# The first stage of a diffusion transformer kernel: an order written out for four queues, and a norm whose modulation enters as ScalarE's scale and bias

## The chip, the cores and the metric

The kernel runs on one core of a Trainium2 chip. Time is device time in microseconds (us) of one launch, the median of several runs. The profile is one further execution, taken by the hardware profiler. The core's engines are TensorE (PE in the profile; PEld is its weight load), VectorE (DVE), ScalarE (ACT), GpSimd (POOL) and SyncE (SP, which issues most DMAs). Each has its own queue of instructions that it takes strictly in the order of the program; semaphores join them.

## What is computed

Two blocks of a transformer with adaptive norms, in float32. Each sublayer is preceded by an RMS norm whose result is scaled and shifted by a modulation that is a matrix product of the conditioning vector:

```python
def _rms(t, g):
    y = t32 * lax.rsqrt(jnp.mean(t32 * t32, axis=-1, keepdims=True) + NORM_EPS)
    return y.astype(t.dtype) * g
def _modulate(t, g, shift, scale):
    return _rms(t, g) * (1 + scale) + shift
def _swiglu(h, w13, w2):
    gte, up = jnp.split(h @ w13, 2, axis=-1)
    return (jax.nn.silu(gte) * up) @ w2
...
mod = (jax.nn.silu(c) @ mod_w[i] + mod_b[i]).reshape(bsz, 3, 3, 1, D_MODEL)
lat = lat + 0.5 * mod[:, 0, 2] * _swiglu(_modulate(lat, norm_g[i, 0], mod[:, 0, 0], mod[:, 0, 1]), ffn_w13[i, 0], ffn_w2[i, 0])
```

There are 256 tokens of the sequence (`lat`) and 256 of a context (`cx`) with a modulation of its own; the model width is 1024 and the hidden width of the feed-forward 2816. The sublayers are: feed-forward, convolution mixer, feed-forward; feed-forward, attention, feed-forward.

## The kernel before

**Layout.** Activations are held transposed: 128 partitions of the model width by 512 columns (256 of the sequence, s=0, and 256 of the context, s=1), in eight slices k=0..7. So a modulation is one value per partition for each k and s. Products keep float32 accuracy by splitting: an operand becomes a high part (`hh`, `wh`), rounded to the type that PE takes at full rate, and a low part (`hl`, `wl`), the difference; each product is three matmuls, high by high, high by low and low by high (lines 122 to 124). `split` makes the high part on ACT (L98) and the low part on DVE (L99).

**First stage.** It ends where the fourth block of the first feed-forward's weights starts; it takes three blocks (i=0..2), each with a gate and an up result of 512 columns. Nothing can be multiplied before x has come, its squares are summed, and the first modulation is known. The stage is cut into quarters q=0..3 of two slices k each, so that products can start with the first quarter. The steps in `FIRST_STEPS` are written out for PE:

- `P` ch q (`mod_pe`, L758): the product of the conditioning with 256 columns of the modulation's weights (ch 1 is the scale, ch 0 the shift), in two halves that each wait for their own 512 KB load; then a copy of the row to SBUF on ACT (L763).
- `T` ch q (`mod_turn`, L770): small matmuls that turn the row into columns; DVE adds the bias and writes A00 (scale, L775) or B00 (shift, L775).
- `F` (`fill`, L731): matmuls without use that keep PE busy; `WARM` of them stand at the start.
- `W` i (`first_w`): the load of weight block i and its split in four parts.
- `N` q (`norm_q`): DVE multiplies A00 by the norm's weight (L784); for each k and s DVE makes t = x * A * (1/rms) (L264), ACT makes hh = t + B (L274), DVE makes hl = (t + B) - hh (L275).
- `H` q (`copy_q`): ACT writes the unsplit t + B to `h32` (L798), which sums of halves need later.
- `M` i q: the twelve products of block i with quarter q.
- `S`: the conditioning vectors broadcast over the partitions (`scbc`) and their Silu on ACT.

1/rms over all partitions (`rms_all`, L252, copied by L845) is made ahead of P00. Only PE's order is fixed (`manual_schedule` with PE alone). DVE, ACT and SP get their order from the framework's scheduler.

**Behind it.** `w13_post` makes silu(gate) * up of the three blocks and splits it. `h.sums()` adds and subtracts halves of h32 and splits the results (T1 to T4), which the blocks from 8 on use in place of h (products on sums of halves, seven instead of eight). `tick(n)` gives n units of modulation work to DVE: each (L142) is a row-wise product of a 1024-wide piece of modulation weights with `scbc`. Ticks stand behind every block and every finished output of the second product (`ev` of them each). Blocks 3 to 7 take h as it is (`AS_IS`), in `ffn`. Five constants (`convk`, `qg`, `kg`, `cosT`, `sinT`) are loaded through ACT's DMA queue.

**DMA.** SP issues the loads in its order, and each waits for the one before it on the same of eight semaphores; ACT's loads take from the same eight.

Of the kernel before, what the change touches and what calls it, by code (L numbers as in the profile page):

```python
# [9 lines left out]
F32 = mybir.dt.float32  # L10
# [15 lines left out]
HEADS = 8  # L26
KVH = 2
EPS = 1e-6
WARM = 36
FILL = 8  # L30

FIRST_STEPS = (
    "P10 P00 T10 T00 N0 F W0 M00 W1 P11 P01 T11 T01 N1 H0 M10 W2 M01 P12 H1 M11 P02 T12 T02 "
    "N2 M20 H2 M21 P13 P03 T13 T03 N3 M02 M12 M22 H3 M03 M13 M23 S"
)


# [1 line left out]
def hybrid_kernel(ctx: ExitStack, tc: tile.TileContext, a: dict, out: bass.AP):  # L42
# [53 lines left out]

    def split(hi, lo, src):
        nc.scalar.activation(out=hi, in_=src, func=AF.Copy)  # L98
        nc.vector.tensor_tensor(out=lo, in0=src, in1=hi.bitcast(F32), op=ALU.subtract)  # L99

    def half():

# [515 lines left out]
    def ffn(l, b, h, tot, gate, tail, gs=(), ev=1.5):  # L618
        gs = list(gs)
        i0 = 0  # L620
        for t, n in enumerate(THIRDS):
            between = ()
            if tot == T2:
                heads = []
                if t == 0 and not gs:

                    w = [load_w(a["w13"][l, b, 0])]
                    gs = [new_pair("g") for _ in range(2)]
                    pp = [(psum("pg"), psum("pu")) for _ in range(2)]
                    w13_mm(pp[0], w[0], h, range(KT), 0, S)  # L630
                    flush()
                    w.append(load_w(a["w13"][l, b, 1]))
                    w13_mm(pp[1], w[1], h, range(KT), 0, S)
                    h.sums(0)
                    w13_mm(pp[0], w[0], h, range(KT), S, T2)
                    w13_post(pp[0], gs[0], 0, T2)
                    heads.append(Pair(a["w13"][l, b, 2], h))
                    h.sums(1)
                    heads[0].sums(0)
                    w13_mm(pp[1], w[1], h, range(KT), S, T2)  # L640
                    w13_post(pp[1], gs[1], 0, T2)
                    heads[0].head()
                    h.sums(2)
                    heads[0].sums(1)
                prev = None
                for i in range(len(gs), n):
                    if t == 0 and not heads and i in AS_IS[l, b]:
                        w = load_w(a["w13"][l, b, i])
                        pp = psum("pg"), psum("pu")
                        if prev:  # L650
                            prev.seven()
                        w13_mm(pp, w, h, range(4), 0, T2)
                        if prev:
                            gs.append(new_pair("g"))
                            prev.four(gs[-1])
                            prev = None
                        w13_mm(pp, w, h, range(4, KT), 0, T2)
                        gs.append(new_pair("g"))
                        w13_post(pp, gs[-1], 0, T2)
                        tick(4)  # L660
                        continue
                    if heads:
                        pr = heads.pop(0)
                    else:
                        pr = Pair(a["w13"][l, b, i0 + i], h)
# [12 lines left out]

                def last():
                    gs.append(new_pair("g"))  # L680
                    prev.four(gs[-1])

                between = (prev.seven, last) if prev else ()
            else:
                for i in range(n):
                    w = load_w(a["w13"][l, b, i0 + i])
                    gs.append(new_pair("g"))
                    pp = psum("pg"), psum("pu")
                    w13_mm(pp, w, h, range(KT), 0, tot)
                    w13_post(pp, gs[i], 0, tot)  # L690
                    tick(1)
            i0 += n
            box = {}

            def ws2(m):
                if m // 2 not in box:
                    src = a["w2a"][l, b, m // 2] if t == 0 else a["w2b"][l, b, t - 1, m // 2]
                    box[m // 2] = load_raw(src, 2 * n * P)
                raw = box[m // 2]
                o = (m % 2) * n * P  # L700
                hi, lo = half()
                split(hi[:, : n * P], lo[:, : n * P], raw[:, o : o + n * P])
                return lambda k: (hi[:, k * P : k * P + P], lo[:, k * P : k * P + P])

            cur = gs
            end = t == len(THIRDS) - 1
            project(
                ws2, lambda k, c0, c1: (cur[k][0][:, c0:c1], cur[k][1][:, c0:c1]), n,
                gate, tail if end else None, tot, 2 if end and tot == T2 else 0, ev, between,
            )  # L710
            gs = []
# [32 lines left out]

    rows = {}

    def mod_pe(ch, q):


        raws = []  # L750
        for i in range(2):
            raws.append(hot("pm", F32))
            nc.sync.dma_start(raws[i], a["mod0"][ch, q, :, i * 1024 : i * 1024 + 1024])
        pr = psum("pr") if (ch, q) == (1, 0) else psmall("pr")
        for k in range(KT):
            g = 32 * (k % 4)
# [22 lines left out]
            op=ALU.add,  # L779
        )  # L780

    def norm_q(q):
        k2 = slice(2 * q, 2 * q + 2)
        nc.vector.tensor_tensor(  # L784
            out=A00[:, k2, :], in0=A00[:, k2, :], in1=both(normg[:, 0, 0, k2]), op=ALU.mult
        )
        for k in range(2 * q, 2 * q + 2):
            for s in range(2):
                t = None
                if k % 2:  # L790
                    t = tp.tile([P, T2], F32, name=nm("t"), tag="sg", bufs=3)[:, :S]
                ts[k, s] = norm_k(s, k, h, A00, B00, ris[s], t)

    def copy_q(q):
        for s in range(2):
            h32[q, s] = gp.tile([P, T2], F32, name=nm("hr"), tag="gl" if s else "gh")
            for k in range(2 * q, 2 * q + 2):
                nc.scalar.activation(  # L798
                    out=h32[q, s][:, (k % 2) * S : (k % 2) * S + S], in_=ts[k, s],
                    func=AF.Identity, bias=B00[:, k, s : s + 1],  # L800
                )

    pps = {}
    ris, ts = [], {}

    def first_mm(i, q):
        if q == 0:
            pps[i] = psum("pg"), psum("pu")
        w13_mm(pps[i], ws[i], h, range(2 * q, 2 * q + 2), 0, T2)

    ws, gs0 = {}, []

    def load_sc():
        for v in range(2):
            nc.sync.dma_start(scbc[:, v, :], a["c2"][v : v + 1, :].to_broadcast([P, D]))
            nc.scalar.activation(out=scbc[:, v, :], in_=scbc[:, v, :], func=AF.Silu)

    def first_w(i):
        if i < 2:
            ws[i] = load_w(a["w13"][0, 0, i], fine=True)  # L820
            return
        raw = load_raw(a["w13"][0, 0, i])
        parts = [new_pair("w") for _ in range(4)]
        for j in (0, 2, 1, 3):
            split(*parts[j], raw[:, j * T2 : j * T2 + T2])
        ws[i] = lambda o: tuple(t[:, o % T2 : o % T2 + P] for t in parts[o // T2])

    steps = {
        "P": mod_pe,
        "T": mod_turn,  # L830
        "F": lambda: fill(FILL),
        "H": copy_q,
        "S": load_sc,
        "W": first_w,
        "N": norm_q,
        "M": first_mm,
    }
    with tc.manual_schedule(engines={mybir.EngineType.PE}):
        fill(WARM)
        sums = [rms_sum(s, (accs[s], accs[s, "last"])) for s in range(2)]  # L840
        for step in FIRST_STEPS.split():
            if step == "P00":
                for s in range(2):
                    ris.append(tp.tile([P, S], F32, name=nm("ris"), tag=f"ris{s}", bufs=1))
                    nc.scalar.copy(ris[s], rms_all(*sums[s]))  # L845
            steps[step[0]](*(int(c) for c in step[1:]))
    done[0, 0] = done[0, 1] = 16
    h = FirstBlocks(h, h32)
    for i in range(3):
        gs0.append(new_pair("g"))  # L850
        w13_post(pps[i], gs0[i], 0, T2)
    h.sums()
    tick(4)

    convk = cload("convk", [P, 3, KT])
    qg = cload("qg", [P, 1])
    kg = cload("kg", [P, 1])
    cosT = cload("cosT", [P, S])
    sinT = cload("sinT", [P, S])


    hn = Plain()
    ffn(0, 0, h, T2, lazy_gate(0, 0), tail_norm(0, 1, hn), gs0, 1.8)
    h = hn

    zs = []
# [358 lines left out]
```

## Time and profile before

| | us |
|---|---|
| median of 3 runs | 1588.35 |
| lowest and highest | 1585.33, 1588.66 |
| profiled execution, whole | 1586.51 |
| its span (first to last instruction) | 1584.7 |

The mean granted clock of TensorE over the profiled execution is 0.995 of full speed.

How to read the lines. In the busy times by stretch, the columns are the stretch, its length, then busy us and number of instructions of PE, PEld, DVE, ACT and POOL, then the granted clock of TensorE, the share of the DMA engines and GB/s. In the rows in time, the columns are start, duration, engine, line of the code, operation, result and operands, shapes and count; brackets give idle time before it and what ended it. A matmul of float32 operands shows as two records, one of the rounded type as one; rows of PE last longer than the distance to the next, as matmuls are pipelined. In the groups by shape, the columns behind the count are busy us in all, mean ns of one, and idle us before it with what ended it. In the list of waits they are us in all, times, and the longest.

### The profile page before, as it was taken

The page shows a single profiled execution, that of the slowest core. Times are in us where ns is not written, and L with a number is a line of the kernel's source. Part 1 is how long each engine was busy: PE and PEld are TensorE (multiplying, and loading weights), DVE is VectorE, ACT ScalarE, POOL GpSimd, SP SyncE. Part 2 cuts the span into 40 slices and gives each one's busy share as a digit, 9 for nine tenths or more (in the row PEclk, how much of TensorE's full clock was granted, in tenths as well). Part 3 has the DMA queues.
Part 4 walks back from the last instruction along what each step waited for, and adds up shares of the span by engine and source line. Part 5 has one row for each costly group of instructions (what it writes and reads, how often), then busy time and mean ns, then how long its engine had stood idle before and what let it go on. Part 6 is the DMA issues. An engine that isn't in the chain of part 4 may idle for free.

```text
span 1584.7 us, 25774 instructions
## 1 busy us (share of the span) xinstructions
PE 1565.9 (99%) x10666; PEld 1448.4 (91%) x10666; DVE 1302.0 (82%) x1984; ACT 720.4 (45%) x1103; POOL 26.1 (2%) x20
## 2 busy tenths in 40 slices
PE   9999999999999999999999999999999998999999
PEld 6788998999888899999899899899899897899999
DVE  5988789979988789898898899788898788665554
ACT  6522452545322365335255376245255456543443
POOL 0000000000000000000000000000000004100000
PEclk9999999999999999999999999999999999999999
DMA  9565235334454423442433423532543554355452
GB/s 361 200 221 186 94 137 183 120 132 158 170 205 160 159 81 132 144 151 100 174 139 110 161 87 109 184 135 98 196 147 127 206 190 163 105 199 191 161 202 102
DMA packets 39573, 248.78 MB, mean 157 GB/s; under 512 B 5408, under 2 KB 7200, under 8 KB 14624
## 3 DMA queue, kind: packets, MB, share of 16 engines
q1 hardware_dynamic: 36864, 245.38, 44.1%
q10 hardware_dynamic: 2592, 1.76, 0.4%
q8 instruction: 83, 1.36, 0.3%
q14 instruction: 34, 0.28, 0.1%
HBM read 244.77 MB, written 1.05 MB: 155 GB/s over the span
## 4 chain that ended last, share of the span: by engine, by line
PE 94%; DVE 2%; ACT 2%; DMA 1%; issue 0%; ACTq 0%; DVEq 0%
PE py L123 10%; PE py L124 10%; PE py L122 10%; PE p L124 7%; PE p L123 7%; PE p L122 7%; PE q L122 5%; PE q L124 5%; PE q L123 5%; PE pg L122 3%; PE pg L124 3%; PE pg L123 3%; PE pu L122 3%; PE pu L123 3%; PE pu L124 3%; PE pv L122 1%
## 5 line engine op out<-in xcount | busy, mean ns | idle before, releaser
L98 ACT ACTIVATE wh<-wr 128x1024 fp32r<-128x1024 f32 (+2 forms) x276 | 276.7, 1013 | 374.3 <-PE py L123 123.2
L99 DVE TENSOR_TENSOR wl<-wr,wh 128x1024 fp32r<-128x1024 f32 (+2 forms) x276 | 320.4, 1166 | 94.2 <-ACT wh L98 93.5
L142 DVE CUSTOM_DVE_ANT_0 junk<-wr,scbc,modb 128x1024 bf16<-128x1024 f32 x224 | 286.7, 1280 | 32.8 <-DMA wr<-in_modT 30.2
L122 PE MATMUL py<-gh,wh 128*128 128x512 f32 (+1 forms) x746 | 263.2, 353 | 0.0
L123 PE MATMUL py<-gl,wh 128*128 128x512 f32 (+1 forms) x746 | 263.0, 353 | 0.0
L124 PE MATMUL py<-gh,wl 128*128 128x512 f32 (+1 forms) x746 | 262.8, 352 | 0.0
L124 PEld LDWEIGHTS py<-gh,wl 128*128 128x128 f32 x746 | 141.1, 189 | 19.0
L122 PEld LDWEIGHTS py<-gh,wh 128*128 128x128 f32 x746 | 141.2, 189 | 18.5
L123 PEld LDWEIGHTS py<-gl,wh 128*128 128x128 f32 x746 | 141.2, 189 | 18.2
L99 DVE TENSOR_TENSOR wl<-ws,wh 128x1024 fp32r<-128x1024 f32 x108 | 131.7, 1222 | 26.9 <-ACT wh L98 26.5
L98 ACT ACTIVATE wh<-ws 128x1024 fp32r<-128x1024 f32 x108 | 113.7, 1058 | 79.6 <-PE p L123 33.8
L124 PE MATMUL p<-th,wl 128*128 128x256 f32 x432 | 122.2, 283 | 0.0
L123 PE MATMUL p<-tl,wh 128*128 128x256 f32 x432 | 122.2, 283 | 0.0
L122 PE MATMUL p<-th,wh 128*128 128x256 f32 x432 | 122.2, 283 | 0.0
L453 DVE SCALAR_TENSOR_TENSOR x<-py,G,x 128x256 f32<-128x256 f32 x168 | 74.2, 477 | 27.2 <-PE py L124 27.0
L122 PE MATMUL q<-bh,wh 128*128 128x256 f32 x320 | 90.6, 283 | 0.0
L123 PE MATMUL q<-bl,wh 128*128 128x256 f32 x320 | 90.6, 283 | 0.0
L124 PE MATMUL q<-bh,wl 128*128 128x256 f32 x320 | 90.6, 283 | 0.0
L122 PEld LDWEIGHTS p<-th,wh 128*128 128x128 f32 x432 | 82.9, 192 | 0.3
L123 PEld LDWEIGHTS p<-tl,wh 128*128 128x128 f32 x432 | 82.9, 192 | 0.3
L124 PEld LDWEIGHTS p<-th,wl 128*128 128x128 f32 x432 | 82.9, 192 | 0.0
L122 PE MATMUL pg<-hh,wh 128*128 128x256 f32 (+1 forms) x240 | 76.0, 317 | 2.7 <-ACT wh L98 1.6
(236 smaller groups left out, 4037.3 us busy)
## 6 DMA issues: line engine op xcount, KB each, us to landing
wr<-in_w SPq DMA_DIRECT2D x88, 1024.0 KB, 4.9
wr<-in_modT SPq DMA_DIRECT2D x64, 1024.0 KB, 4.9
wr<-in_w2b SPq DMA_DIRECT2D x32, 896.0 KB, 4.6
wr<-in_w2a SPq DMA_DIRECT2D x16, 1024.0 KB, 4.9
pm<-in_mod SPq DMA_DIRECT2D x16, 512.0 KB, 9.6
wr<-in_cw_cx SPq DMA_DIRECT2D x8, 1024.0 KB, 4.9
wr<-in_cw_b SPq DMA_DIRECT2D x4, 1024.0 KB, 5.9
wr<-in_cw_out SPq DMA_DIRECT2D x4, 1024.0 KB, 4.8
```

Of the source, the lines that this page charges most:

```text
L98: nc.scalar.activation(out=hi, in_=src, func=AF.Copy)
L99: nc.vector.tensor_tensor(out=lo, in0=src, in1=hi.bitcast(F32), op=ALU.subtract)
L122: nc.tensor.matmul(ps, wh, mh, start=first, stop=False, **kw)
L123: nc.tensor.matmul(ps, wh, ml, start=False, stop=False, **kw)
L124: nc.tensor.matmul(ps, wl, mh, start=False, stop=last, **kw)
L142: nc.vector.tensor_tensor_reduce(out=junk, in0=raw[:, j * D : j * D + D], in1=scbc[:, v, :], scale=1.0, scalar=modb[:, l, col : col + 1], ...
L453: nc.vector.scalar_tensor_tensor(out=x[:, m, s * S : s * S + S], in0=ps[:, o : o + S], scalar=g[:, m, s : s + 1], in1=x[:, m, s * S : s * ...
```

## The change

- **Order.** `FIRST_STEPS` is written anew, and `manual_schedule` now holds PE, DVE, ACT and SP: all four take the stage's work in the order of the steps. Loads become steps of their own (`L` for modulation weights, `R` for weight blocks), splits are cut into single parts (`W` i p), and the products of the first two blocks with quarter 0 into single kinds (`h` high by high, `w` with the low weight, `l` with the low activation; arguments block, quarter, slice). The other `M` steps go through each slice as h, w, l, gate and up by turns.
- **Norm.** `U` q: DVE makes x * (norm's weight) * (1/rms) straight into h32, which needs no modulation. `N` q j then makes hh = A * that + B on ACT with scale and bias per partition; the unsplit value in place, for q=0 on DVE (`tensor_scalar`), otherwise on ACT with scale and bias; and hl as a difference of two tensors on DVE. The product of A00 with the norm's weight is gone.
- **Place of other work.** `X` (1/rms) stands between P10 and P00. The two loads of `scbc` come behind all loads of the stage; the constants' loads come behind the Silu of `scbc`. `h.sums()` is called in the first of the blocks of `ffn`, its instructions held behind the last low weight split of block 1. `tick(4)` behind it is gone, and `ev` of the first feed-forward is 2 where it was 1.8.
- **Filler.** `WARM` is 34 where it was 36, `FILL` 4 where it was 8.

```diff
+FIRST_STEPS = (
+    "L10 L00 R0 R1 P10 X U0 L11 P00 L01 T10 T00 W00 N00 W01 N01 F h000 w000 l000 R2 W10 W11 "
+    "h001 w001 h100 h101 l001 l100 l101 W02 W03 U1 P11 L12 P01 L02 T11 T01 w100 w101 N10 N11 "
+    "W12 W13 M01 W20 W21 U2 W22 W23 P12 L13 P02 L03 T12 T02 M11 N20 N21 M20 U3 P13 P03 T13 "
+    "T03 M21 N30 N31 M02 M12 M22 M03 M13 M23 S"
+)
...
+                        if "T1" not in h.t:
+                            with tc.issue_after(rows["W1"]):
+                                h.sums()
                         w13_mm(pp, w, h, range(4), 0, T2)
...
+    def scale_q(q):
+        for s in range(2):
+            h32[q, s] = gp.tile([P, T2], F32, name=nm("hr"), tag="gl" if s else "gh")
         for k in range(2 * q, 2 * q + 2):
             for s in range(2):
...
+                nc.vector.scalar_tensor_tensor(
+                    out=raw_of(k, s), in0=x[:, k, s * S : s * S + S],
+                    scalar=normg[:, 0, 0, k : k + 1], in1=ris[s], op0=ALU.mult, op1=ALU.mult,
+                )
+
+    def norm_one(q, j):
+        k = 2 * q + j
+        hs = [pick(h, k, s * S, s * S + S) for s in range(2)]
+        ab = [(A00[:, k, s : s + 1], B00[:, k, s : s + 1]) for s in range(2)]
         for s in range(2):
...
+            nc.scalar.activation(
+                out=hs[s][0], in_=raw_of(k, s), func=AF.Identity, scale=ab[s][0], bias=ab[s][1]
+            )
+        for s in range(2):
+            r = raw_of(k, s)
+            if q == 0:
+                nc.vector.tensor_scalar(
+                    out=r, in0=r, scalar1=ab[s][0], scalar2=ab[s][1], op0=ALU.mult, op1=ALU.add
+                )
+            else:
                 nc.scalar.activation(
...
+                    out=r, in_=r, func=AF.Identity, scale=ab[s][0], bias=ab[s][1]
                 )
+        for s in range(2):
+            nc.vector.tensor_tensor(
+                out=hs[s][1], in0=raw_of(k, s), in1=hs[s][0].bitcast(F32), op=ALU.subtract
+            )
...
+    queues = [nc.tensor, nc.vector, nc.scalar, nc.sync]
+    with tc.manual_schedule(engines={e.engine for e in queues}):
         fill(WARM)
...
-    h.sums()
-    tick(4)
...
-    ffn(0, 0, h, T2, lazy_gate(0, 0), tail_norm(0, 1, hn), gs0, 1.8)
+    ffn(0, 0, h, T2, lazy_gate(0, 0), tail_norm(0, 1, hn), gs0, 2)
```

In the order that follows from it, ACT takes in quarter 0: the first weight part, hh, hh, a weight part, hh, hh, then two weight parts of block 1 and the other two of block 0; in quarter 1: hh, hh, unsplit, unsplit, twice over, then six weight parts, then the row copies of quarter 2. DVE takes the four units of block 3's tick behind the five sums and ahead of the splits of the sums.

More of the change, by code (lines that the diff above doesn't have):

```diff
@@ L28 @@
 EPS = 1e-6
-WARM = 36
-FILL = 8
+WARM = 34
+FILL = 4
 FIRST_STEPS = (
-    "P10 P00 T10 T00 N0 F W0 M00 W1 P11 P01 T11 T01 N1 H0 M10 W2 M01 P12 H1 M11 P02 T12 T02 "
-    "N2 M20 H2 M21 P13 P03 T13 T03 N3 M02 M12 M22 H3 M03 M13 M23 S"
[4 rows of a table added]
 )
@@ L98, in split @@
         nc.scalar.activation(out=hi, in_=src, func=AF.Copy)
-        nc.vector.tensor_tensor(out=lo, in0=src, in1=hi.bitcast(F32), op=ALU.subtract)
+        return nc.vector.tensor_tensor(out=lo, in0=src, in1=hi.bitcast(F32), op=ALU.subtract)
     def half():
@@ L745, in hybrid_kernel, with mod_load @@
     rows = {}
+    def mod_load(ch, q):
+        rows[ch, q] = [hot("pm", F32) for _ in range(2)]
+        for i in range(2):
+            nc.sync.dma_start(rows[ch, q][i], a["mod0"][ch, q, :, i * 1024 : i * 1024 + 1024])
     def mod_pe(ch, q):
[L750 to L753, printed above, removed]
+        raws = rows[ch, q]
         pr = psum("pr") if (ch, q) == (1, 0) else psmall("pr")
@@ L780, in mod_turn, with first_inv, raw_of @@
         )
[L782 to L786, printed above, removed]
+    def first_inv():
+        for s in range(2):
+            ris.append(tp.tile([P, S], F32, name=nm("ris"), tag=f"ris{s}", bufs=1))
+            nc.scalar.copy(ris[s], rms_all(*sums[s]))
+    def raw_of(k, s):
+        return h32[k // 2, s][:, (k % 2) * S : (k % 2) * S + S]
+    def scale_q(q):
+        for s in range(2):
+            h32[q, s] = gp.tile([P, T2], F32, name=nm("hr"), tag="gl" if s else "gh")
@@ L787, in norm_q @@
         for k in range(2 * q, 2 * q + 2):
             for s in range(2):
[L789 to L794, printed above, removed]
-        for s in range(2):
-            h32[q, s] = gp.tile([P, T2], F32, name=nm("hr"), tag="gl" if s else "gh")
-            for k in range(2 * q, 2 * q + 2):
+                nc.vector.scalar_tensor_tensor(
+                    out=raw_of(k, s), in0=x[:, k, s * S : s * S + S],
+                    scalar=normg[:, 0, 0, k : k + 1], in1=ris[s], op0=ALU.mult, op1=ALU.mult,
+                )
@@ L798, in copy_q @@
                 nc.scalar.activation(
-                    out=h32[q, s][:, (k % 2) * S : (k % 2) * S + S], in_=ts[k, s],
-                    func=AF.Identity, bias=B00[:, k, s : s + 1],
-                )
+                    out=r, in_=r, func=AF.Identity, scale=ab[s][0], bias=ab[s][1]
+                )
+        for s in range(2):
+            nc.vector.tensor_tensor(
+                out=hs[s][1], in0=raw_of(k, s), in1=hs[s][0].bitcast(F32), op=ALU.subtract
+            )
     pps = {}
-    ris, ts = [], {}
+    ris = []
@@ L806, in first_mm, with first_part, part @@
+    def first_part(lo):
+        def part(i, q, j):
+            if (q, j, lo) == (0, 0, 0):
+                pps[i] = psum("pg"), psum("pu")
+            k = 2 * q + j
+            for n in range(2):
+                nc.tensor.matmul(
+                    pps[i][n], ws[i]((1 - n) * 1024 + k * P)[lo == 2],
+                    pick(h, k, 0, T2)[lo == 1],
+                    start=(k, lo) == (0, 0), stop=(k, lo) == (KT - 1, 1),
+                )
+        return part
     def first_mm(i, q):
-        if q == 0:
-            pps[i] = psum("pg"), psum("pu")
@@ L809, in first_mm @@
-        w13_mm(pps[i], ws[i], h, range(2 * q, 2 * q + 2), 0, T2)
-    ws, gs0 = {}, []
+        for j in range(2):
+            for lo in (0, 2, 1):
+                first_part(lo)(i, q, j)
+    ws, gs0, raws, cut = {}, [], {}, {}
     def load_sc():
@@ L815, in load_sc, with first_raw, first_w @@
             nc.sync.dma_start(scbc[:, v, :], a["c2"][v : v + 1, :].to_broadcast([P, D]))
-            nc.scalar.activation(out=scbc[:, v, :], in_=scbc[:, v, :], func=AF.Silu)
-    def first_w(i):
+            last = nc.scalar.activation(out=scbc[:, v, :], in_=scbc[:, v, :], func=AF.Silu)
+        rows["last"] = last.ins
+    def first_raw(i):
+        raws[i] = load_raw(a["w13"][0, 0, i])
         if i < 2:
[L820 to L826, printed above, removed]
+            ts = [half() for _ in range(2)]
+            cut[i] = [tuple(t[:, c : c + T2] for t in ts[j]) for j in range(2) for c in (0, T2)]
+        else:
+            cut[i] = [new_pair("w") for _ in range(4)]
+        ws[i] = lambda o: tuple(t[:, o % T2 : o % T2 + P] for t in cut[i][o // T2])
+    def first_w(i, p):
+        j = (2, 0, 3, 1)[p]
+        ins = split(*cut[i][j], raws[i][:, j * T2 : j * T2 + T2])
+        rows[f"W{i}"] = ins.ins
     steps = {
@@ L831, in hybrid_kernel @@
         "F": lambda: fill(FILL),
-        "H": copy_q,
         "S": load_sc,
+        "L": mod_load,
+        "R": first_raw,
         "W": first_w,
-        "N": norm_q,
+        "X": first_inv,
+        "U": scale_q,
+        "N": norm_one,
+        "h": first_part(0),
+        "l": first_part(1),
+        "w": first_part(2),
         "M": first_mm,
     }
-    with tc.manual_schedule(engines={mybir.EngineType.PE}):
+    queues = [nc.tensor, nc.vector, nc.scalar, nc.sync]
+    with tc.manual_schedule(engines={e.engine for e in queues}):
         fill(WARM)
@@ L841, in hybrid_kernel @@
         for step in FIRST_STEPS.split():
[L842 to L845, printed above, removed]
             steps[step[0]](*(int(c) for c in step[1:]))
@@ L851, in hybrid_kernel @@
         w13_post(pps[i], gs0[i], 0, T2)
-    h.sums()
-    tick(4)
[L855 to L859, printed above, removed]
+    with tc.issue_after(rows["last"]):
+        convk = cload("convk", [P, 3, KT])
+        qg = cload("qg", [P, 1])
+        kg = cload("kg", [P, 1])
+        cosT = cload("cosT", [P, S])
+        sinT = cload("sinT", [P, S])
     hn = Plain()
-    ffn(0, 0, h, T2, lazy_gate(0, 0), tail_norm(0, 1, hn), gs0, 1.8)
+    ffn(0, 0, h, T2, lazy_gate(0, 0), tail_norm(0, 1, hn), gs0, 2)
     h = hn
```

## The prediction

> **What bounds the kernel now.** I read the page first (busy shares, chain of waits), then the busy times by stretch, PE's rows in time over the first 70 us, and the durations by shape.
>
> ```profile
> PE 1565.9 (99%) x10666; PEld 1448.4 (91%) x10666; DVE 1302.0 (82%) x1984; ACT 720.4 (45%) x1103; POOL 26.1 (2%) x20
> ...
> PE 94%; DVE 2%; ACT 2%; DMA 1%; issue 0%; ACTq 0%; DVEq 0%
> ...
> 0.00:23.00 23.00, 19.91 (x153) 17.08 (x153) 9.33 (x31) 12.14 (x24) 0.19 (x4) 0.93 0.89 323
> 23.00:68.00 45.00, 44.20 (x267) 32.36 (x268) 38.06 (x78) 32.17 (x63) 0.00 (x0) 1.00 0.67 266
> 68.00:400.00 332.00, 331.99 (x2122) 303.39 (x2123) 292.13 (x437) 136.81 (x202) 0.00 (x0) 1.00 0.45 156
> ```
>
> PE sets the end: 94% of the chain is PE, and from 68 us on it has no hole in the stretch shown. The change keeps every product, so it can win only before PE's work becomes gapless. That is the first stage, from the span's start to the first product of the fourth block of weights (67.36 below). Its 23 us before the first product are startup; its 44 us after are products with the modulation's own small matmuls between.
>
> ```profile
> 14.16 0.64 PE L758 MATMUL pr<-pm,sccol 128*32 128x256 f32 x8 [0.31 <-DMA pm<-in_mod]
> 14.73 1.66 PE L252 MATMUL ss<-ident,ri 128*128 128x128 f32 x8
> 16.32 1.94 PE L758 MATMUL pr<-pm,sccol 128*32 128x256 f32 x16
> 18.18 1.25 PE L770 MATMUL pr<-rowsum,row 128*128 128x2 f32 x8
> 19.30 2.03 PE L731 MATMUL idle<-ones 128*128 128x128 f32 x16
> 22.95 0.50 PE L122 MATMUL pg<-hh,wh 128*128 128x512 f32 x1 [1.62 <-ACT wh L98]
> ...
> 40.24 1.07 PE L758 MATMUL pr<-pm,sccol 128*32 128x256 f32 x16
> 41.24 1.22 PE L770 MATMUL pr<-rowsum,row 128*128 128x2 f32 x8
> 42.32 0.48 PE L122 MATMUL pg<-hh,wh 128*128 128x512 f32 x1
> ...
> 50.91 0.48 PE L122 MATMUL pg<-hh,wh 128*128 128x512 f32 x1
> ...
> 67.36 0.39 PE L122 MATMUL pg<-hh,wh 128*128 128x512 f32 x1
> ```
>
> From 50.91 to 67.36 PE runs 72 products: 0.2285 us each. A P step is 1.00 us (40.24 to 41.24), a pair of T steps 1.08 (41.24 to 42.32). So the stage's PE work after 22.95 is 144 products (32.9), six P (6.0) and three pairs of T (3.2): 42.1 of 44.4 us. The 2.3 us left are waits and the change of shape between groups, which I take as 0.09 on either side.
>
> **The change part by part.** *First product.* Before, PE waited 1.62 us for a weight split that stood behind three hh and one hr on ACT:
>
> ```profile
> 19.10 0.16 DVE L775 TENSOR_TENSOR A<-pr,sb 128x4 f32<-128x4 f32 x1 [5.32 <-PE pr L770]
> ...
> 19.96 0.15 DVE L775 TENSOR_TENSOR mod<-pr,modb 128x4 f32<-128x4 f32 x1
> 20.15 1.31 ACT L274 ACTIVATE hh<-t,mod 128x256 fp32r<-128x256 f32 x3 [1.41 <-DVE mod L775]
> 21.76 1.13 ACT L98 ACTIVATE wh<-wr 128x512 fp32r<-128x512 f32 x2
> ```
>
> Now the split W00 stands ahead of hh, and x times 1/rms times the weight (U0, four instructions of 0.48, by the L264 row below) runs on DVE where A had waited 5.32 us. Between A, B and the first product remain B (0.15) and two hh. The five constants' DMAs go behind load_sc; they had cost the weights' queue a wait of 4.6 us and ACT five issues:
>
> ```profile
> SPq L94 <- DMA qg<-in_qg: 4.6, 1, 4.6
> ...
> 10.00:12.00 2.00, 1.87 (x17) 1.68 (x17) 1.62 (x5) 1.61 (x3) 0.00 (x0) 1.00 0.84 244
> 12.00:14.00 2.00, 1.85 (x20) 1.35 (x19) 0.33 (x2) 1.15 (x3) 0.00 (x0) 1.00 0.72 264
> 14.00:16.00 2.00, 1.84 (x16) 1.43 (x16) 0.00 (x0) 0.74 (x2) 0.00 (x0) 0.80 1.00 382
> 16.00:18.00 2.00, 2.00 (x18) 0.64 (x17) 0.00 (x0) 0.37 (x1) 0.00 (x0) 0.50 0.99 396
> 18.00:20.00 2.00, 2.00 (x18) 1.82 (x15) 0.77 (x4) 0.37 (x1) 0.00 (x0) 0.84 1.03 408
> ```
>
> The last column falls to 244 and 264 GB/s from 10 to 14 us where it is near 400 later; with the queue full the second half of P10 should not wait, so X starts at 14.1 instead of 14.73. Then 1.6 (X), 1.94 (P00, at the reduced clock of 16 to 18 us) and 1.25 (T): T ends at 18.9, B at 19.1. If the DMA gives nothing, 0.5 later. FILL of 4 (half of 2.03 us) ends near 20.0, in front of nothing late.
>
> The new hh carries a scale and a bias read per partition, which no row of this shape shows. Neighbours:
>
> ```profile
> L220 ACT ACTIVATE sq<-x 128x256 f32<-128x256 f32 x24 | 9.9, 412 | 10.7 <-DVE x L453 10.7
> L274 ACT ACTIVATE hh<-t,mod 128x256 fp32r<-128x256 f32 x56 | 25.4, 500 | 17.9 <-DVE t L264 11.9 <-DVE mod L775 5.5 <-ACT hh L274 0.2
> L938 ACT ACTIVATE sq<-pq 128x512 f32<-128x512 f32 x4 | 2.4, 592 | 1.8 <-PE pq L124 1.8
> L948 ACT ACTIVATE kn<-pq,qg 128x512 f32<-128x512 f32 x4 | 2.7, 684 | 0.0
> L1081 ACT ACTIVATE e<-psc,nb,scq 128x512 f32<-128x512 f32 x16 | 12.4, 777 | 7.0 <-DVE nb L1075 4.6 <-POOL pn L1089 2.3
> ```
>
> None, one and two such operands give 592, 684 and 777 ns; one step is 0.09. So the new hh takes 0.59. Three old ones in 1.31 follow each other every 0.41; I take 0.50 for the new ones, between 0.41 (operand reads hidden) and 0.59 (no overlap). Hence B 19.1, hh at 19.15 and 19.65 to 20.25, first product at 20.3: 2.65 us earlier (2.1 without the DMA).
>
> *What the opening gives back.* PE's order is now h, w, l, and DVE must make, after the second hh (20.25), two raw copies, two lo halves and the second wl before the fourth product:
>
> ```profile
> L264 DVE SCALAR_TENSOR_TENSOR t<-x,A,ris 128x256 f32<-128x256 f32 x16 | 7.2, 478 | 0.2
> L228 DVE TENSOR_TENSOR acc<-acc,sq 128x256 f32<-128x256 f32 x66 | 25.0, 418 | 2.0 <-ACT sq L220 1.7
> L887 DVE TENSOR_SCALAR d<-u,convk 128x512 f32<-128x512 f32 x8 | 3.8, 480 | 0.0
> L99 DVE TENSOR_TENSOR wl<-wr,wh 128x512 fp32r<-128x512 f32 x12 | 7.7, 685 | 0.4 <-ACT wh L98 0.4
> L99 DVE TENSOR_TENSOR wl<-wr,wh 128x1024 fp32r<-128x1024 f32 x200 | 243.5, 1220 | 68.3 <-ACT wh L98 67.6
> ...
> L142 DVE CUSTOM_DVE_ANT_0 junk<-wr,scbc,modb 128x1024 bf16<-128x1024 f32 x224 | 286.7, 1280 | 32.8 <-DMA wr<-in_modT 30.2
> ```
>
> One raw of 0.35 (half the columns of the 0.480 row; 0.2 and 0.48 are its bounds, 0.3 us either way in the stall) and two lo of 0.42, each overlapping the next by 0.08, then 0.685: 20.25 + 0.4 + 0.7 + 0.65 = 22.0. Unhindered the fourth product would start at 21.0: a stall of 1.0.
>
> *Quarter 1.* T01 is followed on PE by four products (w100, w101) and the twelve of M01. ACT makes hh, hh, raw, raw twice: eight at 0.50 are 4.1 us after B, then a lo half 0.42; the last pair of M01 can start 0.3 + 4.6 = 4.9 us after T01. The fourteen products before it take 3.3. Stall 1.6 (0.9 to 2.3 with the spacing's bounds). The old chain had only t and hh there and the raw copies behind.
>
> *Quarters 2 and 3.* T12 waits for its row copy behind six weight splits on ACT: about 0.4. After T02 stand 24 products, the next P and T, and 12 more: 11.3 us over the 4.1 of ACT plus some 2 us of DVE splits; after T03 stand 48 products, 10.9 us. Hidden; without that cover each would cost a stall like quarter 1's.
>
> *Sum.* 20.3 + 42.1 + three groups at 0.18 (0.5) + stalls 1.0, 1.6, 0.4 and 0.3 (row copies before each T, 0.09 each) = 66.2, against 67.36: **1.1 us earlier**; by the bounds 64.9 to 67.5.
>
> *Behind the stage.* SP takes the two scbc loads behind P13 and P03; ACT does table load, two Silu and five DMA issues before th, sg and the wh of block 3; DVE does five sums, four units of modulation and four tl before gm and the two wl. These are in queue order, so what is late holds all behind it. From the last lo half (near 52) DVE needs the last three of the five sums (1.8), four units at 1.28, four tl (2.4): 61.3. M03 ends 24 products before 66.2, at 60.7, so sg lets gm start at 61.3 as well. gm, tl, wl, gl, gm, wl at 0.6, 0.6, 1.15, 0.6, 0.6, 1.15 (the 0.685 and 1.220 rows less the overlap) end at 66.0; the third product of block 3 needs it at 66.7. Margin 0.7: no cost, but little room. The tick(4) taken out (four units, 5.1 us of DVE) returns as 24 finishes at 2 instead of 1.8. After 68 us DVE is busy 292 of 332 us: room for it. Products of later blocks keep their number; some change places, which I price at 0, plus or minus 1 us, by the longest wait that a late stage shows:
>
> ```profile
> PE ss L237 <- DVE acc L228: 1.2, 1, 1.2
> ```
>
> **Rivals.** *(a) The stalls vanish.* If the new hh run every 0.41 us and the opening is covered, the stage is start plus work, 20.3 + 42.6 = 62.9, or 4.5 us earlier; half of it, 3.3, is likelier than all. For it: ACT overlaps neighbours in the 1.31 row. Against it: DVE's opening chain has no slack.
>
> *(b) The weight tile comes late: slower.* W00 is ahead of hh in ACT's order, so hh waits for the first weight tile. Before, no wait for it showed at 21.76, which only says that it had landed by then. By the GB/s rows 5.4 MB are in by 16.5 us with a full queue, so I put it at 18; the point from which it decides is 18.5. At 21.7 the first product is at 21.7 + 0.62 + 1.1 + 0.1 = 23.5, 3.2 later than forecast: stage end 69.4, 2.1 us slower than before.
>
> *(c) The clock.* The granted clock was 0.80, 0.50 and 0.84 from 14 to 20 us: 3.4 us at half clock, behind the row sums and waits of 11 to 14. The filler is now half as long, and the first ten products come with holes. If the clock is still low for another such time, the loss is half of it, 1.7 us: 0.6 us slower than before. Against it: P00, T and F are 4.2 us on end.
> [...]
>
> *(d) Late stages.* Another place of the same products leaves PE a longer wait near the end, with a drop of the clock behind it:
>
> ```profile
> 1380.00:1420.00 40.00, 36.62 (x277) 35.85 (x277) 29.52 (x51) 19.53 (x34) 0.00 (x0) 0.91 0.62 215
> ```
>
> There PE idles 3.4 us and 9% of the clock is gone (3.6 us). One more such place costs up to 5, net 4 us slower. Only the order speaks for it.
>
> **How the numbers follow.** The profiled execution took 1586.51 us (span 1584.7 and 1.8 around it); the forecast by it is 1585.4. The three runs' median, 1588.35, lies 1.8 above it, with 1585.33 as lowest; the mean of the four is 1587.2. I forecast from that mean, 1587.2 - 1.1 = 1586.1. Chances: forecast 0.60, (a) 0.22, (b) 0.07, (c) 0.05, (d) 0.06. In time (a) is 1582.7 to 1584, (b) 1589.3, (c) 1587.8, (d) 1591. The range 1582.7 to 1589.5 leaves out (d) and the far end of (a). 0.2%, 3.2 us, is about what a measurement of this kernel tells from no change. Faster by more: (a), and a little of the forecast since the runs scatter by 3.3 us: 0.25. Slower by more: (d) and some scatter of (b): 0.08. Within: 0.67.
>
> **What would show it.** First product at 20.3 (22.95 before); PE waits in M01 for hh and hl, near 1.6 us in all; hh of 0.59, spaced 0.50; block 3's first product near 66.2; no DMA wait on the second half of P10. A first product after 22 speaks for (b); a clock below 1.00 after 20 us for (c); new PE waits after 1,200 us for (d). The forecast is wrong if block 3 starts before 65 or after 67.5, or if anything after 68 us moves the end by more than 1 us.

## The result, and the profile after

| | before | after |
|---|---|---|
| median of 8 runs each, us | 1587.01 | 1590.76 |
| lowest to highest | 1584.71 to 1588.66 | 1588.69 to 1593.65 |
| profiled execution, span | 1584.7 | 1590.0 |

The ratio after to before is 1.0024, with a 95% interval from 1.0014 to 1.0033: 3.8 us slower. Forecast were 1.1 us faster, and a range that ends at 1589.5.

The page after gives the busy shares and the chain of waits.

```profile
PE 1568.6 (99%) x10654; PEld 1451.5 (91%) x10654; DVE 1302.5 (82%) x1984; ACT 719.1 (45%) x1099; POOL 26.0 (2%) x20
...
PE 91%; DVE 5%; ACT 2%; DMA 2%; issue 0%; SPq 0%; ACTq 0%; DVEq 0%
```

DVE's work is the same (1302.5 us; 1302.0 before), but its share of the chain went from 2% to 5%: more of what PE waits for now ends on DVE.

**The stage.** Busy times by stretch, and PE's rows in time, after the change:

```profile
0.00:23.00 23.00, 20.43 (x146) 17.55 (x147) 11.46 (x37) 13.74 (x26) 0.19 (x4) 0.94 0.93 353
23.00:68.00 45.00, 43.76 (x268) 32.74 (x267) 35.45 (x70) 30.89 (x58) 0.00 (x0) 0.99 0.66 253
68.00:400.00 332.00, 331.99 (x2121) 303.07 (x2120) 294.39 (x441) 136.36 (x203) 0.00 (x0) 1.00 0.44 155
```

```profile
15.36 1.07 PE L767 MATMUL pr<-pm,sccol 128*32 128x256 f32 x16
16.36 1.21 PE L779 MATMUL pr<-rowsum,row 128*128 128x2 f32 x8
17.43 1.14 PE L738 MATMUL idle<-ones 128*128 128x128 f32 x8
20.09 0.61 PE L841 MATMUL pg<-hh,wh 128*128 128x512 f32 x1 [1.52 <-ACT hh L814]
20.61 0.80 PE L841 MATMUL pu<-hh,wh 128*128 128x512 f32 x1
...
66.32 0.39 PE L126 MATMUL pg<-hh,wh 128*128 128x512 f32 x1
```

The first product starts at 20.09 (22.95 before), block 3 at 66.32 (67.36 before): 1.0 us were won here. But the first products last 0.6 to 0.8 us instead of 0.5, as TensorE's clock is halved from 20.3 to 23.8 us. Before, the half clock lay ahead of the first product (0.50 from 16 to 18 us). From 20 to 24 us, before and then after:

```profile
20.00:24.00 4.00, 2.31 (x15) 1.68 (x15) 4.00 (x11) 3.85 (x9) 0.00 (x0) 1.00 1.01 413
```

```profile
20.00:24.00 4.00, 3.90 (x9) 2.44 (x10) 4.00 (x11) 3.62 (x8) 0.00 (x0) 0.57 1.04 420
```

ACT's rows in time show what the first product waited for:

```profile
18.43 0.63 ACT L102 ACTIVATE wh<-wr 128x512 fp32r<-128x512 f32 x1 [1.52 <-DMA wr<-in_w]
18.96 1.08 ACT L814 ACTIVATE hh<-hr,mod,A 128x256 fp32r<-128x256 f32 x2
```

The weight tile, not the modulation, holds the two hh: it landed at 18.4.

**Behind the stage.** Four places in both kernels' rows of PE, before and then after: the end of the convolution, the end of the second feed-forward, attention's first transposition, the last feed-forward's first product.

```profile
567.23 0.38 PE L237 MATMUL ss<-ones,sq 128*128 128x1 f32 x2 [0.52 <-ACT sq L220]
...
918.03 0.38 PE L237 MATMUL ss<-ones,sq 128*128 128x1 f32 x2 [0.63 <-ACT sq L220]
...
1325.46 0.66 PE L1098 MATMUL pt<-ident,pn 128*128 128x128 f32 x4 [0.42 <-POOL pn L1089]
...
1388.27 0.58 PE L122 MATMUL pg<-hh,wh 128*128 128x256 f32 x1 [1.11 <-ACT hh L274]
```

```profile
566.81 0.38 PE L241 MATMUL ss<-ones,sq 128*128 128x1 f32 x2 [0.52 <-ACT sq L224]
...
920.23 0.38 PE L241 MATMUL ss<-ones,sq 128*128 128x1 f32 x2 [0.73 <-ACT sq L224]
...
1330.82 0.66 PE L1147 MATMUL pt<-ident,pn 128*128 128x128 f32 x4 [0.54 <-POOL pn L1138]
...
1393.60 0.58 PE L126 MATMUL pg<-hh,wh 128*128 128x256 f32 x1 [1.41 <-ACT hh L278]
```

After minus before goes from -1.04 (block 3) to -0.42, +2.20, +5.36 and +5.33. So 6.4 us were lost in many places from 280 to 1,330 us, none of them in the stage. Three kinds of loss can be seen. The smallest stands from 279 to 300 us, where products of two results alternate and some of them start up to 0.14 us late: 0.8 us in all. The second is waits. The list of PE's waits behind 66 us (us in all, times, the longest), some of the lines that grew, before and then after:

```profile
PE ss L237 <- ACT sq L220: 1.6, 3, 0.6
...
PE pt L1098 <- POOL pn L1089: 1.0, 2, 0.6
...
PE pt L1098 <- DVE ptl L99: 0.7, 2, 0.4
```

```profile
PE ss L241 <- ACT sq L224: 2.6, 4, 1.2
PE pt L1147 <- POOL pn L1138: 2.3, 3, 0.9
PE pt L1147 <- DVE ptl L103: 1.8, 3, 1.0
...
PE q L126 <- ACT wh L102: 0.5, 1, 0.5
PE q L128 <- DVE wl L103: 0.5, 1, 0.5
```

The whole list sums to 11.3 us before and 13.9 after. The `ss` line grew in name only: its wait of 1.2 us stands before as well, in a line of its own (`PE ss L237 <- DVE acc L228`, in the prediction). By place, PE's rows in time give 1.06 us of new waits near 603 us, 0.55 near 920, 0.7 in attention and 0.2 elsewhere. The two lines for q are new. DVE's rows at that place, before and then after, and PE's:

```profile
598.42 0.68 DVE L570 TENSOR_TENSOR ws<-wr,ws 128x512 f32<-128x512 f32 x1
599.02 1.27 DVE L142 CUSTOM_DVE_ANT_0 junk<-wr,scbc,modb 128x1024 bf16<-128x1024 f32 x1
...
600.83 1.21 DVE L99 TENSOR_TENSOR wl<-ws,wh 128x1024 fp32r<-128x1024 f32 x1
```

```profile
600.14 1.28 DVE L146 CUSTOM_DVE_ANT_0 junk<-wr,scbc,modb 128x1024 bf16<-128x1024 f32 x1
...
601.35 0.69 DVE L574 TENSOR_TENSOR ws<-wr,ws 128x512 f32<-128x512 f32 x1
601.95 1.28 DVE L146 CUSTOM_DVE_ANT_0 junk<-wr,scbc,modb 128x1024 bf16<-128x1024 f32 x1
...
603.16 1.22 DVE L103 TENSOR_TENSOR wl<-ws,wh 128x1024 fp32r<-128x1024 f32 x1
```

```profile
603.18 0.39 PE L126 MATMUL q<-th,wh 128*128 128x256 f32 x1 [0.54 <-ACT wh L102]
...
604.44 0.39 PE L128 MATMUL q<-th,wl 128*128 128x256 f32 x1 [0.52 <-DVE wl L103]
```

The sum ws at L570 before is the one at L574 after. Before, one modulation unit (junk) stands behind it and in front of its split wl; after, one stands in front of ws and another behind it. The weight sums come late by one unit, and PE waits 1.06 us. Nothing in the stage touches this place: the unit has moved.

The third is the clock. Busy times by stretch around 568 us, in stretches of 3.41 us counted from where each profile's clock changes, before and then after:

```profile
564.75:568.16 3.41, 2.78 (x24) 2.61 (x22) 2.73 (x7) 3.41 (x7) 0.00 (x0) 1.00 0.00 0
568.16:571.58 3.42, 2.73 (x20) 2.53 (x21) 2.42 (x3) 1.14 (x2) 0.00 (x0) 1.00 0.03 5
```

```profile
566.51:569.92 3.41, 2.32 (x16) 2.03 (x17) 2.74 (x4) 2.37 (x4) 0.00 (x0) 0.99 0.00 0
569.92:573.34 3.42, 3.42 (x18) 3.42 (x18) 0.24 (x1) 0.00 (x0) 0.00 (x0) 0.51 0.58 189
```

Both kernels have the same two waits there, 0.52 and 0.68. Before, they fall into two stretches, each some 80% busy, and the clock stays; after, into one stretch, 68% busy, and the next 3.4 us run at half clock: 1.7 us lost. Near 925 us after has two such stretches on end (clock 0.50 from 921.46 to 928.28) and before one (919.75 to 923.16); together these make 3.4 of the 5.3 us between the two profiles. But that is this pair of executions. Over 33 runs of before and 8 of after the mean granted clock is the same, 0.994, so the clock does not explain the medians. The small stops and the new waits, 3.3 us together, come near the 3.8 us between the medians.

### The profile page after: what moved, and what is told of

Its sections match the earlier page's. It is cut to its first block, busy times and chain, and to the rows that moved or that the text cites. A ratio compares the mean times of both kernels' runs of the same rounds, so it can differ in the third digit from the quotient of the medians.

```text
span 1590.0 us, 25721 instructions
## 1 busy us (share of the span) xinstructions
PE 1568.6 (99%) x10654; PEld 1451.5 (91%) x10654; DVE 1302.5 (82%) x1984; ACT 719.1 (45%) x1099; POOL 26.0 (2%) x20
## 4 chain that ended last, share of the span: by engine, by line
PE 91%; DVE 5%; ACT 2%; DMA 2%; issue 0%; SPq 0%; ACTq 0%; DVEq 0%
PE py L126 9%; PE py L127 9%; PE py L128 9%; PE p L126 6%; PE p L127 6%; PE p L128 6%; PE q L126 5%; PE q L128 5%; PE q L127 5%; PE pg L126 2%; PE pg L127 2%; PE pg L128 2%; PE pu L127 2%; PE pu L126 2%; PE pu L128 2%; DVE wl L103 1%
## 5 line engine op out<-in xcount | busy, mean ns | idle before, releaser
L126 PEld LDWEIGHTS py<-gh,wh 128*128 128x128 f32 x746 | 141.2, 189 | 18.4
L102 ACT ACTIVATE gh<-gm 128x512 fp32r<-128x512 f32 (+1 forms) x88 | 50.7, 576 | 55.8 <-DVE gm L619 44.2
```

What stands on the lines that cost most here:

```text
L126: nc.tensor.matmul(ps, wh, mh, start=first, stop=False, **kw)
```

## The experiments

Theory: the modulation units cost it. `tick(4)` and the 1.8 set, with the fractions carried on, on which output each later unit falls, and with it the order of products on PE and of DVE's work to the end. Rivals: the new stage itself (its queues, the late constants, the filler and its clock); chance. In the table, owed is the count of units asked for by the end of the first feed-forward: 20 from blocks 3 to 7, 7 from the paired blocks, 24 outputs at the rate given, and 4 where `tick(4)` stands. PE's order is read from the traces, by the result that each product goes to: in the first feed-forward behind block 3 two orders occur (1 and 2), behind it three (A, B and C). Waits is the sum of PE's list of waits behind 66 us in the profile. e1 to e12 have 11 or 12 runs each, against 33 or 35 of before.

| | stage | rate, owed | PE's order | waits | median | ratio to before (95%) |
|---|---|---|---|---|---|---|
| before | old | 1.8, 74.2 | 1 A | 11.3 | 1587.1 to 1587.5 | |
| after | new | 2, 75.0 | 2 B | 13.9 | 1590.76 | 1.0024 (1.0014 to 1.0033) |
| e1 | new | 1.8, 74.2 | 1 A | 12.2 | 1586.88 | 0.9999 (0.9989 to 1.0009) |
| e2 | old | 2, 75.0 | 2 B | 16.1 | 1592.65 | 1.0031 (1.0017 to 1.0045) |
| e3 | new | 1.8, 70.2 | 1 A | 11.1 | 1586.92 | 0.9995 (0.9987 to 1.0004) |
| e4 | new, long filler | 2, 75.0 | 2 B | 14.1 | 1591.05 | 1.0016 (1.0004 to 1.0028) |
| e5 | new | 1.8, 74.2 + 0.4 | 1 B | 14.6 | 1589.30 | 1.0012 (1.0003 to 1.0020) |
| e6 | new | 2, 75.0 - 0.8 | 2 A | 12.3 | 1588.58 | 1.0008 (0.9998 to 1.0018) |
| e7 | new | 1.8, 74.2 - 0.4 | 1 A | 11.1 | 1586.97 | 0.9996 (0.9986 to 1.0005) |
| e8 | new | 1.9, 72.6 | 1 C | 11.0 | 1585.11 | 0.9986 (0.9977 to 0.9995) |
| e9 | new, long filler | 1.9, 72.6 | 1 C | 11.2 | 1584.88 | 0.9981 (0.9972 to 0.9990) |
| e10 | as e8 | 1.9, 72.6 | 1 C | 11.3 | 1585.32 | 0.9982 (0.9973 to 0.9991) |
| e11 | old | 1.9, 72.6 | 1 C | 13.0 | 1587.93 | 0.9998 (0.9989 to 1.0006) |
| e12 | old | 1.8, 74.2 + 0.4 | 1 B | 14.2 | 1590.48 | 1.0020 (1.0010 to 1.0030) |

**Units undone, units alone (e1, e2).** Edit of e1, against after; e2 makes the opposite edit of the same two places in the kernel before.

```diff
         w13_post(pps[i], gs0[i], 0, T2)
+    tick(4)
...
-    ffn(0, 0, h, T2, lazy_gate(0, 0), tail_norm(0, 1, hn), gs0, 2)
+    ffn(0, 0, h, T2, lazy_gate(0, 0), tail_norm(0, 1, hn), gs0, 1.8)
```

> The kernel after the change, with the four units (tick(4)) put back behind the products of the first stage and 1.8 units for each finished output in the first feed-forward; the new first stage stays. Its products stand, behind the stage, in the order of the kernel before. Theory (the loss comes from where the modulation units stand behind the stage): the new stage's gain of 1.0 us is left, 1587.0 - 1.0 = 1586.0 (1585 to 1587.2); PE's waits behind 68 us sum to about 11.3 us as before (13.9 after), with none for q near 603 us. Rival (the new stage itself, by its queues or late constants, costs it): unchanged at 1590.8. [...]

> The kernel before, with nothing changed but the units: tick(4) taken out and 2 units for each finished output instead of 1.8. Its products stand, behind the stage, in the order of the kernel after. Theory (units): 1587.0 + 2.6 us of waits + 0.7 us of small stops near 290 us, and up to 3.4 us of clock: 1590.3 to 1593.7, so about 1591.8, which is after's time plus the 1.0 us that only the new stage gains. Rival (the stage costs it): 1587.0, within 0.8.

e1 has the new stage and is at before's time; e2 has the old stage and is slower than before by more than after is. The loss comes with the units and goes with them. PE's waits in e1 (12.2) are nearer to 11.3 than to 13.9, and none is for q near 603. The gain of 1.0 us does not show in e1: 0.9999, with room for some 1.6 us in either direction. In e2 one wait more appears, at the end of the old stage, which the new one does not have:

```profile
68.88 0.50 PE L124 MATMUL pg<-hh,wl 128*128 128x512 f32 x1 [1.55 <-DVE wl L99]
```

**Which of the two (e3).** e1's second edit alone: 1.8, and `tick(4)` still out.

> The kernel after, with 1.8 units for each finished output as before and tick(4) still out: a third order, in which PE's products stand as before but for 24 places, while the units on DVE stand four places late. Theory (what counts is the order of PE's products that follows from the units): near 1586.5 (1585.5 to 1588). Second form of the theory (what counts is that DVE's units come late at all): 1590 to 1592. Rival (the stage): 1590.8.

The first form held: 1586.92. Four units fewer at the start cost nothing. What costs here is the order that follows from the rate of 2; in e3 PE takes its results in the order of before.

**The filler (e4).**

```diff
-WARM = 34
-FILL = 4
+WARM = 36
+FILL = 8
```

> The kernel after, with the filler matmuls of before (36 and 8 instead of 34 and 4); the order of all else is unchanged. Rival clock (the half clock from 20.3 to 23.8 us is due to the filler taken out): the first products run at full clock, 1.7 us faster, 1589.1. Theory (units): 1590.8, within 0.8, as the four matmuls more, 1 us, delay the first product a little at most; the time at half clock only moves.

The half clock at 20 us is gone (1.00 from 20 to 24 us), block 3 starts at 65.98, and the kernel is still slower than before: the later loss is not the opening's. Whether the filler wins something stays open. The median, 1591.05, shows no gain; the ratio is 1.3 us below after's, and its interval holds both the theory's forecast and the rival's.

**The carry (e5, e6, e7).** One line behind the first feed-forward; e5 and e7 in e1 with + 0.4 and - 0.4, e6 in after with - 0.8:

```diff
     ffn(0, 0, h, T2, lazy_gate(0, 0), tail_norm(0, 1, hn), gs0, 1.8)
+    owed[0] += 0.4
```

> The kernel of e1 (new stage, four units put back, 1.8 per output) with one line more: behind the first feed-forward the count of units owed is raised by 0.4, so that later units fall one output earlier here and there. PE's products stand as before up to the end of the first feed-forward, and exactly as in the kernel after from there on. Theory (the later order costs it, by the fraction of a unit that is carried): the two profiles differ behind 320 us by 5.7 us, 3.4 of it clock, so e1 + 2.3 = 1589.2 (1588 to 1590.5), with PE's waits on wh and wl for q near 603 us back (0.5 each). Rival (the number of units in the first feed-forward, or the order there, costs it): 1586.9 as e1, within 0.8.

> The kernel after, with one line more: behind the first feed-forward the count of units owed is lowered by 0.8, the carry that the kernel before has there. The first feed-forward stands as in the kernel after; behind it stands another order, near that of before. Theory: only the loss within the first feed-forward is left (0.8 us of small stops near 290 us), plus or minus what this other order does: 1587.7 (1586.5 to 1589), with no wait of q near 603 us. Rival (the first feed-forward's units cost it): 1590.8 as after.

> The kernel of e1 with the count of units owed lowered by 0.4 behind the first feed-forward: in the first feed-forward the order of before, behind it PE's order of e6. Theory: e6 less 0.8 us, 1586.9 (1585.5 to 1588.3). Rival (any change of the carry costs, since the orders of before were the lucky ones): 1589 or more, as e5.

All three lie in the theory's ranges: 1589.30, 1588.58 and 1586.97. In e5, where the first feed-forward is as before and only what follows is as after, q's waits are back, in PE's rows in time:

```profile
601.60 0.39 PE L126 MATMUL q<-th,wh 128*128 128x256 f32 x1 [0.55 <-ACT wh L102]
...
602.86 0.39 PE L128 MATMUL q<-th,wl 128*128 128x256 f32 x1 [0.51 <-DVE wl L103]
```

e6 and e7 have no such line. They differ by the first feed-forward alone, by 1.6 us of median (0.8 expected; each median is uncertain by about 1). Some 0.7 of it goes with the mean clock of their runs, 0.9933 in e6 and 0.9942 in e7: a line through 101 runs of before gives 0.83 us for 0.001.

With order A, DVE's own order behind the first feed-forward takes three forms (before and e1; e3; e6 and e7), and with 1 A the medians stay within 1586.9 to 1587.5. So another place of the units on DVE alone cost nothing in these, and e7 is no test of another order on PE. In B the orders of PE and DVE changed together; which of the two counts for how much is not shown.

**Another rate (e8), and again (e10); with the filler (e9).** e8 is after with 1.9 in place of 2.

> The kernel after with 1.9 units for each finished output of the first feed-forward instead of 2 (1.8 in e3): a carry of its own, and PE changes its target less often than in the kernel after (1158 times to 1196; e1 and e3 1163, before 1068). Theory (a lottery of orders): between 1585.5 and 1590.8, likeliest near e3's 1586.9 by the number of changes. Rival (the rate itself counts, half-way between e3 and after): 1588.9.

> The kernel of e8 once more, beside e9 on one chip. 1585.1 if e8's order is better than that of before; 1586.5 to 1587 if it was only the best of several draws.

> The kernel of e8 with the filler matmuls of before (36 and 8). In seven profiles with the new stage and the short filler the clock was halved for 3.4 to 6.8 us from about 20 us on and block 3 began at 66.3 to 68.2 us, 67.1 in the mean; in e4, the one with the long filler, no half clock before 560 us and 65.98. Theory (rival (c) of the prediction holds for the short filler): block 3 near 66.0, no half clock in the opening, and 1585.1 - 1.1 = 1584.0. Rival (the filler takes what the clock gives): 1585.1.

e8 and e10 agree: with this order the new stage makes a kernel 2 to 3 us faster than before, and 5 to 6 faster than after. e8 came out 0.4 below its theory's range. Why it beats before is known only in part: its waits are just 0.3 us fewer, and 0.8 to 1.1 us go with the clock, whose mean is 0.9958 in e8 and 0.9952 in e10 (0.9945 and 0.9942 in the runs of before beside them). In DVE's rows at the place of q, e8 has no unit between the sums and their splits:

```profile
598.22 0.68 DVE L574 TENSOR_TENSOR ws<-wr,ws 128x512 f32<-128x512 f32 x1
598.93 0.69 DVE L578 TENSOR_TENSOR ws<-wr,ws 128x512 f32<-128x512 f32 x1
600.21 2.36 DVE L103 TENSOR_TENSOR wl<-ws,wh 128x1024 fp32r<-128x1024 f32 x2 [0.59 <-ACT wh L102]
```

That keeps it clear of after's wait there, but does not set it apart from before: e6 and e7 have the same rows, and with its one unit before has no wait there either.

The filler's effect on the clock can be seen from 20 to 24 us, first in e9, then in e10:

```profile
20.00:24.00 4.00, 3.00 (x11) 1.94 (x12) 4.00 (x11) 4.00 (x8) 0.00 (x0) 1.00 1.02 412
```

```profile
20.00:24.00 4.00, 3.22 (x7) 2.02 (x8) 4.00 (x11) 4.00 (x9) 0.00 (x0) 0.50 1.02 410
```

Clock 1.00 against 0.50, and block 3 at 65.84 against 68.00; yet the medians differ by 0.4 us only, and 1584.88 is nearer to the rival's 1585.1 than to 1584.0. Whether the filler is worth 1 us or nothing stays open: the runs of e9 lie up to 5.5 us apart, those of e10 4.4.

**The order of e8 with the old stage (e11), and the carry with nothing else (e12).** e11 is before without `tick(4)` and with 1.9; e12 is before with e5's one line.

> The kernel before with tick(4) taken out and 1.9 units for each finished output; its products stand, behind the stage, in the order of e8. Theory (order alone): e8's 1585.1, plus 0.3 for the old stage, and up to 1.5 more if block 3 waits for its wl as in e2: 1585.4 to 1586.9. Rival (e8's gain is the new stage's): 1587.2.

> The kernel before with one line more and nothing else: the count of units owed raised by 0.4 behind the first feed-forward. No work is added or taken away; PE's products stand from there on as in the kernel after. Theory (the later order, made by the carry): 1587.2 + 2.3 = 1589.5 (1588.5 to 1591). Rival (a fraction of a unit can't cost anything): 1587.2.

e11 missed its range by 1.0, with a median near the rival's 1587.2: order C alone does not make the gain. Nor does the new stage alone, as e1, e3 and e7 have it and gain nothing that can be told. In e11 the row of its block 3 shows a wait that e8 does not have:

```profile
69.56 0.50 PE L124 MATMUL pg<-hh,wl 128*128 128x512 f32 x1 [1.91 <-DVE wl L99]
```

Without `tick(4)` the old stage's DVE takes gl and gm of the first blocks ahead of this split, which starts at 68.28 (67.60 in e2; in the new stage of the kernel after it starts at 65.33 and is done in time). e12 is the plainest proof of the theory: no work is changed, one count is raised by 0.4, and the kernel is 3.2 us slower, with the same two waits for q in its list:

```profile
PE q L122 <- ACT wh L98: 0.5, 1, 0.5
PE q L124 <- DVE wl L99: 0.5, 1, 0.5
```

## Why the prediction was wrong

1. **The step that failed** is the sentence "Products of later blocks keep their number; some change places, which I price at 0, plus or minus 1 us". The order behind the stage is worth 3.8 us between after and e3, whose stage is the same, and 3.2 between e12 and before. Its size had been taken from the longest late wait (1.2 us) as if one place moved. In fact the order changes at many places, each worth 0.1 to 1 us, and the sum counts: some 2.5 us more of waits and 0.8 of small stops. Waits of 11.0 to 12.2 go with medians up to 1587.5, waits of 13.9 and more with 1589.3 to 1592.7 (e6 and e11 lie between).
2. **The units.** "The tick(4) taken out returns as 24 finishes at 2 instead of 1.8" was right by count (75.0 to 74.2 units) and wrong as an argument: DVE's room for the work (292 of 332 us busy) says nothing of a unit that stands in front of a weight split which PE needs next.
3. **Rival (d)** had the right kind and, with 1591, the right time, but a chance of 0.06, since "only the order speaks for it". The kind was another order, but the time fits by luck: it expected one wait near the end with a drop of the clock behind it. The loss starts near 280 us, with the small stops, and goes on at 603, 918 and in attention.
4. **The first product**, 20.3 forecast and 20.09 measured, was right by luck: two errors cancel. P00 ran at full clock (1.07 us, not 1.94) and T ended at 17.6, not 18.9; then the weight tile came at 18.43, not 18.0, and hh had to wait for it. That is rival (b), with a point of decision (18.5) that assumed the late B.
5. **Rival (c)** came true as well, and had 0.05. In the new stage with the short filler eight of eight profiles have half clock for 3.4 or 6.8 us from 20 to 22 us on (the mean clock from 20 to 24 us is 0.50 to 0.76); with the long one (e4, e9) neither of two has (1.00 there). The old stage has one such stretch in each of four profiles, at 15.2 (before), ahead of 20 (e2, mean clock 0.91 from 0 to 20 us), at 23.1 (e11) and 23.7 us (e12). In after's profile PE stands still from 18.6 to 20.1 in front of the first product (a wait of 1.52). So block 3 starts at 66.3 to 68.2 in those eight, 67.2 in the mean; with the old stage at 67.36, 66.71, 67.03 and 67.29 in four, 67.1 in the mean; with new stage and long filler at 65.98 and 65.84. The forecast's 66.2 met after's profile (66.32), which is the best of the eight, so that it met was luck. As a mean, the stage as changed gains nothing, and 1.2 us with before's filler.
6. **Smaller terms.** hh took 0.59 and came every 0.49 (0.59 and 0.50 forecast). The opening gave back 2.1 us, not 1.0, with the half clock in it: its twenty products, 4.6 us at 0.2285, took from 20.09 to 26.73. Quarter 1 stalled 0.9, not 1.6 (0.42 for hh, 0.25 and 0.24 for hl), T12 0.32 (0.4). DVE's margin for block 3 was 0.2, not 0.7: its wl ends at 66.55, and the product that needs it is at 66.77. It held.

## What to carry to other kernels

Where a scheduler places background work from running counts, a change of a rate or of a start time can reorder work far behind it: compare the instruction order far from the edit, and price that by running the kernel with the count shifted by a fraction and no work changed (here plus 0.4 gave plus 3.2 us). Judge an edit to one stage by that stage's end in several executions, and apart from the order that it leaves behind. Here the same new stage made a kernel 3.8 us slower than before with a rate of 2, and 2 to 3 us faster with 1.9.

## What the runs showed of the hardware

In the profiles of before and after, between 28 and 1,570 us, the clock dropped without any long idle time. Seven times it went from 1.00 to 0.50: at 919.75, 1332.76 and 1387.38 us before, and at 569.88, 921.46, 1337.88 and 1392.50 after. In the 3.41 us ahead of each, PE was busy 72, 46 and 56% before, and 67, 75, 43 and 45% after; the longest hole inside them was 1.14 us. Other such stretches at full clock were followed by none, as the one from 1380.55 before (71% busy) and the one from 1344.71 after (70%). Each time the half clock lasted 3.41 or 6.83 us. Within each of the two profiles the starts of these drops lie whole multiples of 3.4133 us apart, to 3 ns (103 from 569.88 to 921.46), so the same two waits can fall into one stretch or into two, as at 568 us above.

The clock goes with most of the scatter from run to run (its correlation with the time is -0.77 over 101 runs of before, 60% of the variance); what makes it differ is not shown. Of these runs the 12 with a mean granted clock of 0.992 have a median of 1589.1, the 17 with 0.996 one of 1586.2. So some 3 us between single profiles of this kernel tell nothing by themselves.

PE took the rounded type faster than float32. In the profile of before, at full clock and with weights of 128 by 128, eight float32 matmuls of 128 columns (the filler from 19.30) came every 0.22 us, and products of 512 columns of the rounded type every 0.2285 (50.91 to 67.36): 1.7 and 0.45 ns a column.
